# Two blocks in float32 by split operands: where the low part of the down projections' weights is made

## Chip, cores and metric

One core of one Trainium2 chip. The metric is the device time of one execution in microseconds, from the hardware profiler; two executions of the kernel before gave 1640.35 and 1642.58 us, their median is 1641.46 us.

## What is computed

256 tokens of 1024 channels go through two blocks. The first has a gated feed-forward layer, a hybrid mixer (attention in a window and pooled means), a second feed-forward layer and a gated embedding, each with an RMS norm ahead and behind. The second has two rounds of feed-forward, mixer (gated linear attention in the first round, retention in the second) and feed-forward, each followed by a layer norm. Six of these layers are the same feed-forward, with a hidden width of 2816:

```python
def swiglu(x, w_gate, w_up, w_down):
    return (jax.nn.silu(x @ w_gate) * (x @ w_up)) @ w_down

for i in range(DEPTH_2):
    h = layer_norm(DN_ALPHA * h + 0.5 * swiglu_2(h, ffn_w_in[i, 0], ffn_w_out[i, 0]), ln_g[i, 0], ln_b[i, 0])
    ...
    h = layer_norm(DN_ALPHA * h + 0.5 * swiglu_2(h, ffn_w_in[i, 1], ffn_w_out[i, 1]), ln_g[i, 2], ln_b[i, 2])
```

The loop is the second block's, whose `swiglu_2` is the same with gate and up in one matrix. All data is float32, and so is the result.

## The kernel before

**Split operands.** The matmuls take float32r operands, to which a copy rounds. Each float32 operand is therefore two tiles: a high part, the operand rounded to float32r, and a low part, the operand minus its high part. A product is three matmuls into the same PSUM tile: high by high, high of the tokens by low of the weight, low of the tokens by high of the weight (`mm3`, lines 173 to 177). Each has 128 rows, 128 columns of tokens and 512 columns of weight.

**Weights.** They come from HBM in 275 units of 128 x 2048 float32 (1 MB), in the order of `all_units`. `fetch` (line 143) makes one unit ready: SP starts the load into a `raw` tile (L154), ScalarE writes the rounded copy to `whi` (L155), VectorE writes `raw - whi` to `wlo` (L156). There are 4 `raw` tiles and 5 each of `whi` and `wlo` (`BUFS`, line 94); a tile is written again once the last reader of its former content is done. A feed-forward layer has 12 units of gate, 10 of up and 11 of down, which stand one behind another in the plan; the six layers' down units (`f1d`, `f2d`, `s0d` to `s3d`) are 66 of the 275. They are called d0 to d10 here.

**Down projection** (`lagged`, line 296). The tokens are two blocks of 128, t = 0 and t = 1. Unit i of down is used for t = 0 in step i and for t = 1 three units later (`LAG = 3`): step i does 12 matmuls of t = 0 on unit i, then 12 of t = 1 on unit i-3. So four units are held at any time and the fifth tile is the only one that can be filled ahead. The last two units' work for t = 1 comes at the very end. `after(0)`, the norm of the first block of tokens and the transposes for the next layer, follows t = 0's last step and lies beside the rest of t = 1's products; then comes `after(1)`.

**Order of work.** The source calls `fetch` for unit i+1 when unit i is taken up (`unit`, line 159). The tile framework takes the source's order as priority only: when the program is built it goes through it with durations of its own and writes down for each engine, TensorE too, what can start next by these. So an engine's queue is not always in the source's order; on the chip the queues are fixed, and each engine takes its own strictly in order. Waits are put in by the framework where one engine needs what another wrote, or overwrites what another reads.

**GpSimd** has only small work: parts of the norms (L204, L205, L219, L281) and some element-wise products of the mixers. It starts no DMA in this kernel. The framework keeps a scratch for DMA descriptors of GpSimd's, which is set to 1024 bytes per partition (`dynamic_dma_scratch_size`, line 1011).

Of the kernel before, what the change touches and what calls it, by code (L numbers as in the profile page):

```python
# [11 lines left out]
F32 = mybir.dt.float32  # L12
# [3 lines left out]
ALU = mybir.AluOpType  # L16
# [18 lines left out]
AHEAD = 2  # L35
TURN = (5, 7)


class Split:
    """A float32 operand as two float32r tiles that add up to it exactly."""  # L40

# [7 lines left out]
def ffn_units(g, u, d):  # L49
    """Five chunks of 512 columns of gate and up; their last 256 columns share gate's last two units."""  # L50
    out = []
    for c in range(5):
        out += [(g, 2 * c), (g, 2 * c + 1), (u, 2 * c), (u, 2 * c + 1)]
    return out + [(g, 10), (g, 11)] + [(d, i) for i in range(11)]
# [11 lines left out]
def all_units():  # L66
    """Every weight unit in the order of its use."""
    p = ffn_units("f1g", "f1u", "f1d")
    p += chunk_units("bin", MIX_ORDER) + [("bpl", 0), ("bat", 0), ("bpl", 1), ("bat", 1)] + [("bout", i) for i in range(4)]
    p += ffn_units("f2g", "f2u", "f2d")  # L70
    p += [("pgate", i) for i in range(4)] + [("pproj", 0)]
    p += ffn_units("s0g", "s0u", "s0d")
    p += chunk_units("gin", GLA_ORDER) + [("gout", i) for i in range(4)]
    p += ffn_units("s1g", "s1u", "s1d") + ffn_units("s2g", "s2u", "s2d")
    p += chunk_units("rin", RET_ORDER) + [("rout", i) for i in range(8)]
    return p + ffn_units("s3g", "s3u", "s3d")


class Build:
# [4 lines left out]

# [1 line left out]
    def open(self, ctx):  # L86
# [31 lines left out]
    def const(self, name, i, n=CW, dt=F32):  # L118
        """Piece i of a constant, [128, n]."""
        c = self.T("ld", [P, CW], dt, name=name)  # L120
        self.nc.sync.dma_start(out=c[:, :n], in_=self.ins[name][i])
        return c[:, :n]

# [1 line left out]
    def tick(self):  # L125
        """Six products of 512 columns have gone out: what waited for them follows."""
        self.clock += 1
        while self.later and self.later[0][0] <= self.clock:
            self.later.pop(0)[2]()

    def defer(self, n, fn):
        """Issue fn after n more ticks."""
        self.seq += 1
        self.later.append((self.clock + n, self.seq, fn))
        self.later.sort(key=lambda e: e[:2])

    def settle(self, done):
        """Issue what waits until done()."""
        while not done():
            self.later.pop(0)[2]()  # L140

# [1 line left out]
    def fetch(self, fine=False):  # L143
        """The plan's next unit, on its way to be split."""
        nc = self.nc
        name, i = self.plan[len(self.ready)]
        raw = self.T("raw", [P, UNIT], F32)
        hi = self.T("whi", [P, UNIT], F32R)
        lo = self.T("wlo", [P, UNIT], F32R)
        parts = 4 if fine else 1  # L150
        n = UNIT // parts
        for j in range(parts):
            s = slice(j * n, (j + 1) * n)
            nc.sync.dma_start(out=raw[:, s], in_=self.ins[name][i][:, s])  # L154
            nc.scalar.copy(hi[:, s], raw[:, s])  # L155
            nc.vector.tensor_tensor(out=lo[:, s], in0=raw[:, s], in1=hi[:, s].bitcast(F32), op=ALU.subtract)  # L156
        self.ready.append(Split(hi, lo))

    def unit(self, name, i, kb, ahead=1):
        """Unit i of a weight, on chip and split, as kb rows of blocks."""  # L160
        assert self.plan[self.taken] == (name, i), (name, i, self.plan[self.taken])
        self.taken += 1
        self.ahead(ahead)
        w = self.ready[self.taken - 1]
        self.ready[self.taken - 1] = None
        v = lambda x: x.rearrange("p (k n) -> p k n", k=kb)
        return Split(v(w.hi), v(w.lo))
# [10 lines left out]

# [1 line left out]
    def transpose4(self, src, n=4, name="tp"):  # L180
        """src: [128, n*128] in SBUF -> PSUM [128, n*128], each block transposed."""
        ps = self.TP(name)
# [4 lines left out]
    def split(self, src, n=4, name="xT"):  # L187
        """[128, n*128] -> Split of [128, n, 128]."""
        hi = self.S([P, n, P], F32R, name + "h")
# [8 lines left out]

# [1 line left out]
    def rpow(self, v, eps, n=1, name="r"):  # L200
        """(v + eps) ** -0.5"""
        e = self.small(n, "e" + name)
# [5 lines left out]
    def sumsq(self, srcs, scale):  # L208
        """Sum over the row of (scale * src) ** 2, each source on its own."""
        st = self.small(len(srcs), "ss")  # L210
# [15 lines left out]

# [1 line left out]
    def row_rstd(self, t):  # L228
# [3 lines left out]
    def rms_in(self, t, gpre):  # L232
        """The next layer's operand from h[t]: h * g, transposed and split, and its rstd."""
        nc, h = self.nc, self.h[t]
# [8 lines left out]
    def turn_in(self, xT, t, n, u):  # L243
        """xT[n] becomes u's transpose, once u is about to be there."""
        self.defer(TURN[t] + n, lambda: xT.__setitem__(n, self.splitT(u)))

    def rms_post(self, t, acc, gpost, half):
        """h[t] += (0.5 if half else 1) * rms_norm(acc) * g"""
        nc, h = self.nc, self.h[t]
# [8 lines left out]
    def ln_post(self, t, acc, g, b, half, last=False):  # L258
        """h[t] = layer_norm(ALPHA * h + (0.5 if half else 1) * acc) * g + b; its transpose, split."""
        nc, h = self.nc, self.h[t]  # L260
# [22 lines left out]

# [1 line left out]
    def proj(self, ps, x, w, n=CW, kb=4, k0=0, nk=None):  # L285
        """ps[128, n] += x @ w for one block of tokens; x: list of Split [128, 4, 128], w: list of units
        from row of blocks k0 on, of nk in all."""
        nk = nk or kb * len(w)
# [7 lines left out]
    def lagged(self, x, name, n_units, after, lag=LAG, have=None, extra=None):  # L296
        """[256, K] @ [K, 1024], the first block of tokens ahead of the second by `lag` units of two rows
        of blocks. after(t, acc) follows each block's end; extra: what else follows a step."""
        lag = min(lag, n_units)
# [84 lines left out]
    class Chunks:  # L384
        """x @ w in chunks of 512 columns, issued in pieces of half a unit: a chunk's end calls done(c, t, ps).
        The first two chunks go block of tokens by block of tokens, the others unit by unit."""

# [33 lines left out]

# [1 line left out]
    def mixer(self, xT, r, after):  # L423
# [134 lines left out]

# [1 line left out]
    def ple(self, xT, r, gpost, after):  # L560
# [27 lines left out]

# [1 line left out]
    def gla(self, xT, after):  # L590
# [90 lines left out]
        def inner(t):  # L681
            """The weights of a block of tokens on itself: within each chunk, and of its second chunk on its first."""
            ps, over = self.M("sT"), self.TP("sTo")
# [12 lines left out]
        def far():  # L696
            """The first block's keys decayed to its end, and the second block's queries from its start."""
            e = v3(E1[0])[:, :, P - 1:].to_broadcast([P, H, C])
# [7 lines left out]
        def carry(hp):  # L706
            """What the first block of tokens leaves to the second, for a pair of heads."""
            ps = self.M("kv")
# [36 lines left out]

# [1 line left out]
    def ret(self, xT, after):  # L747
# [76 lines left out]

# [1 line left out]
    def run(self, ctx):  # L826
# [7 lines left out]

        # the first operand comes transposed; its gain is a scalar of each row
        g0 = self.T("g0", [P, KD])
# [28 lines left out]
        def rms_layer(body, post, half, pre):  # L865
            """One residual layer of block 1; the next one's operands."""
            g = {}
# [45 lines left out]
def units(w, kb, n):  # L913
    """[K, N] -> [units, 128, kb * n]: columns outer, rows inner."""
    k, nn = w.shape
# [4 lines left out]
def units_ff(g, u):  # L920
    """Units of gate and of up; the last 256 columns of both make the last two of gate's."""
    last = np.concatenate([g[:, 2560:], u[:, 2560:]], 1)
# [3 lines left out]
def constants():  # L926
    """What depends on shapes alone."""
    out = {"ident": np.eye(P, dtype=np.float32)}
# [25 lines left out]
def bias_windows(rpb):  # L954
    """[8, 15, 31] -> [(t, pair, a), 128 queries, (j, 256 keys)], NEG outside of the window."""
    cols = np.arange(64)
# [65 lines left out]
```

## Time and profile before

| | us |
|---|---|
| two executions, and their median | 1642.58, 1640.35; 1641.46 |
| span of the profiled execution, first to last instruction | 1639.3 |
| TensorE busy with matmuls | 1622.8 |
| VectorE busy | 935.0, of it 632.4 in L156 |
| ScalarE busy | 723.9, of it 526.9 in L155 |
| GpSimd busy | 131.1 |

The median lies 2.2 us above the profiled span. A duration in the rows is from the instruction's start to its end; a matmul's row is longer than the distance to the next one, as they overlap. "Idle before" is the time that the engine had nothing under way, with what ended it.

### The profile page before, as it was taken

The page shows a single profiled execution, that of the slowest core. Times are in us where ns is not written, and L with a number is a line of the kernel's source. Part 1 is how long each engine was busy: PE and PEld are TensorE (multiplying, and loading weights), DVE is VectorE, ACT ScalarE, POOL GpSimd, SP SyncE. Part 2 cuts the span into 40 slices and gives each one's busy share as a digit, 9 for nine tenths or more (in the row PEclk, how much of TensorE's full clock was granted, in tenths as well). Part 3 has the DMA queues.
Part 4 walks back from the last instruction along what each step waited for, and adds up shares of the span by engine and source line. Part 5 has one row for each costly group of instructions (what it writes and reads, how often), then busy time and mean ns, then how long its engine had stood idle before and what let it go on. Part 6 is the DMA issues. An engine that isn't in the chain of part 4 may idle for free.

```text
span 1639.3 us, 18199 instructions
## 1 busy us (share of the span) xinstructions
PE 1622.8 (99%) x7512; PEld 1339.8 (82%) x7512; DVE 935.0 (57%) x809; ACT 723.9 (44%) x712; POOL 131.1 (8%) x149
## 2 busy tenths in 40 slices
PE   8999999999999999999999999999999999999997
PEld 6888878888888888888888888888887888888886
DVE  6644665565453864537747544654538666485444
ACT  6443554454443754333644433443424444344331
POOL 0000200020000300003011000100003300010000
PEclk9999999999999999999999999999999999999999
DMA  9754654545454564546535454555445544364540
GB/s 356 266 184 154 227 210 143 180 176 210 178 193 158 210 229 177 205 146 214 190 138 213 175 203 149 192 223 206 165 169 206 215 154 166 142 240 172 204 150 30
DMA packets 49650, 308.09 MB, mean 188 GB/s; under 512 B 6032, under 2 KB 7056, under 8 KB 14880
## 3 DMA queue, kind: packets, MB, share of 16 engines
q1 hardware_dynamic: 49568, 306.94, 51.6%
q8 instruction: 59, 0.97, 0.2%
q14 instruction: 23, 0.19, 0.0%
HBM read 305.86 MB, written 1.05 MB: 187 GB/s over the span
## 4 chain that ended last, share of the span: by engine, by line
PE 96%; DVE 2%; issue 1%; ACT 0%; DMA 0%; POOL 0%; DVEq 0%; POOLq 0%; SPq 0%
PE mm L175 21%; PE mm L177 21%; PE mm L176 20%; PE acc L177 9%; PE acc L175 9%; PE acc L176 9%; PE hT L184 2%; DVE wlo L156 1%; PE xT L184 1%; PE tp L184 1%; PE sc L464 1%; PE o L487 0%; DVE bn L265 0%; DVE h L264 0%; PE sT L795 0%
## 5 line engine op out<-in xcount | busy, mean ns | idle before, releaser
L156 DVE TENSOR_TENSOR wlo<-raw,whi 128x2048 fp32r<-128x2048 f32 (+1 forms) x287 | 632.4, 2209 | 481.4 <-ACT whi L155 481.3
L155 ACT CAST whi<-raw 128x2048 fp32r<-128x2048 f32 (+1 forms) x287 | 526.9, 1841 | 558.6 <-PE mm L177 283.3
L175 PE MATMUL mm<-whi,xTh 128*128 128x512 f32 x1296 | 516.4, 398 | 0.0
L177 PE MATMUL mm<-whi,xTl 128*128 128x512 f32 x1296 | 506.0, 391 | 0.5 <-DVE xTl L193 0.5
L176 PE MATMUL mm<-wlo,xTh 128*128 128x512 f32 x1296 | 505.0, 390 | 0.0
L177 PEld LDWEIGHTS mm<-whi,xTl 128*128 128x128 f32 x1296 | 243.2, 188 | 53.3 <-DVE xTl L193 1.3
L175 PEld LDWEIGHTS mm<-whi,xTh 128*128 128x128 f32 x1296 | 243.4, 188 | 50.5 <-issue 2.7
L176 PEld LDWEIGHTS mm<-wlo,xTh 128*128 128x128 f32 x1296 | 243.8, 188 | 47.6
L175 PE MATMUL acc<-whi,hTh 128*128 128x512 f32 x528 | 207.4, 393 | 0.0
L177 PE MATMUL acc<-whi,hTl 128*128 128x512 f32 x528 | 205.7, 390 | 0.0
L176 PE MATMUL acc<-wlo,hTh 128*128 128x512 f32 x528 | 205.6, 389 | 0.0
L177 PEld LDWEIGHTS acc<-whi,hTl 128*128 128x128 f32 x528 | 99.1, 188 | 20.7
L176 PEld LDWEIGHTS acc<-wlo,hTh 128*128 128x128 f32 x528 | 99.2, 188 | 20.1
L175 PEld LDWEIGHTS acc<-whi,hTh 128*128 128x128 f32 x528 | 99.1, 188 | 19.8
L193 DVE TENSOR_TENSOR hTl<-hT,hTh 128x512 fp32r<-128x512 f32 (+1 forms) x72 | 46.3, 643 | 58.8 <-ACT hTh L192 58.8
L175 PE MATMUL mm<-whi,xh 128*128 128x512 f32 x176 | 70.5, 401 | 6.6 <-ACT whi L155 6.6
L176 PE MATMUL mm<-wlo,xh 128*128 128x512 f32 x176 | 69.6, 395 | 0.0
L177 PE MATMUL mm<-whi,xl 128*128 128x512 f32 x176 | 69.4, 394 | 0.0
L204 POOL TENSOR_SCALAR erl<-mv 128x1 f32<-128x1 f32 x12 | 5.1, 423 | 771.5 <-DVE mv L267 771.5
L344 ACT ACTIVATE sg<-mm 128x512 f32<-128x512 f32 (+1 forms) x48 | 26.9, 560 | 86.9 <-issue 56.6
L219 POOL TENSOR_TENSOR v<-ss 128x1 f32<-128x1 f32 x16 | 16.2, 1016 | 529.3 <-ACT jk L213 529.3
L192 ACT CAST hTh<-hT 128x512 fp32r<-128x512 f32 (+1 forms) x72 | 39.3, 546 | 26.0 <-PE hT L184 26.0
(216 smaller groups left out, 1267.4 us busy)
## 6 DMA issues: line engine op xcount, KB each, us to landing
raw<-in_rin SPq DMA_DIRECT2D x24, 1024.0 KB, 4.8
raw<-in_bin SPq DMA_DIRECT2D x16, 1024.0 KB, 4.8
raw<-in_f2g SPq DMA_DIRECT2D x12, 1024.0 KB, 4.8
raw<-in_s0g SPq DMA_DIRECT2D x12, 1024.0 KB, 4.9
raw<-in_gin SPq DMA_DIRECT2D x12, 1024.0 KB, 4.8
raw<-in_s1g SPq DMA_DIRECT2D x12, 1024.0 KB, 4.8
raw<-in_s2g SPq DMA_DIRECT2D x12, 1024.0 KB, 4.8
raw<-in_s3g SPq DMA_DIRECT2D x12, 1024.0 KB, 4.8
```

The lines of the kernel that those rows point to most:

```text
L155: nc.scalar.copy(hi[:, s], raw[:, s])
L156: nc.vector.tensor_tensor(out=lo[:, s], in0=raw[:, s], in1=hi[:, s].bitcast(F32), op=ALU.subtract)
L175: mm(ps, x.hi, w.hi, start=start, stop=False)
L176: mm(ps, x.hi, w.lo, start=False, stop=False)
L177: mm(ps, x.lo, w.hi, start=False, stop=stop)
L184: self.nc.tensor.transpose(ps[:, i * P:(i + 1) * P], src[:, i * P:(i + 1) * P], self.ident)
L192: self.nc.scalar.copy(hi, v)
L193: self.nc.vector.tensor_tensor(out=lo, in0=v, in1=hi.bitcast(F32), op=ALU.subtract)
L204: self.nc.gpsimd.tensor_scalar(out=e, in0=v, scalar1=1.0, scalar2=eps, op0=ALU.mult, op1=ALU.add)
L219: self.nc.gpsimd.tensor_tensor(out=v, in0=st[:, 0:1], in1=st[:, 1:2], op=ALU.add)
L344: nc.scalar.activation(sg[:, :n], ps_g[:, :n], AF.Silu)
L464: nc.tensor.matmul(ps[:, j * SEQ:(j + 1) * SEQ], qT[t][64 * a:64 * a + 64, 2 * b + j, :], kT[b][64 * a:64 * a + 64, j, :], start=True, sto ...
```

## The change

Down units no longer take VectorE's subtraction. SP loads `raw` and ScalarE writes `whi` as before. Then a second ScalarE pass writes minus `whi` to `wlo`, and GpSimd starts a DMA from `raw` to `wlo` (both on chip, 1 MB) that adds what it reads to what lies there. All other units are made as before. Removed comments and docstrings change nothing; lines behind the edit move by up to 8.

```diff
 TURN = (5, 7)
+DOWN = ("f1d", "f2d", "s0d", "s1d", "s2d", "s3d")
...
     def fetch(self, fine=False):
...
         raw = self.T("raw", [P, UNIT], F32)
         hi = self.T("whi", [P, UNIT], F32R)
         lo = self.T("wlo", [P, UNIT], F32R)
+        if name in DOWN:
+            nc.sync.dma_start(out=raw, in_=self.ins[name][i])
+            nc.scalar.copy(hi, raw)
+            nc.scalar.activation(lo, hi.bitcast(F32), AF.Copy, scale=-1.0)
+            nc.gpsimd.dma_start(out=lo.bitcast(F32), in_=raw, accum_op=ALU.add)
+            self.ready.append(Split(hi, lo))
+            return
         parts = 4 if fine else 1
```

## Rows read from the trace of the kernel before

**Rows 1.** The profile's page: span, and engines' busy time, share, instructions.

```profile
span 1639.3 us, 18199 instructions
...
PE 1622.8 (99%) x7512; PEld 1339.8 (82%) x7512; DVE 935.0 (57%) x809; ACT 723.9 (44%) x712; POOL 131.1 (8%) x149
```

**Rows 2.** Waits of TensorE: who for whom, us in total, times, longest.

```profile
PE mm L175 <- ACT whi L155: 6.6, 1, 6.6
PE xT L184 <- DVE y L276: 1.1, 3, 0.4
PE mm L177 <- DVE xTl L193: 0.5, 1, 0.5
```

**Rows 3.** Groups by shape: the split of whole units; busy us, mean ns.

```profile
L156 DVE TENSOR_TENSOR wlo<-raw,whi 128x2048 fp32r<-128x2048 f32 x271 | 622.2, 2299 | 479.9 <-ACT whi L155 479.8
L155 ACT CAST whi<-raw 128x2048 fp32r<-128x2048 f32 x271 | 517.7, 1913 | 554.3 <-PE mm L177 283.3 <-PE acc L177 212.6 <-issue 42.1
```

**Rows 4.** Timeline of ScalarE around the first down projection: start, us, instruction.

```profile
119.28 1.91 ACT L155 CAST whi<-raw 128x2048 fp32r<-128x2048 f32 x1 [5.62 <-PE mm L177]
122.04 1.91 ACT L155 CAST whi<-raw 128x2048 fp32r<-128x2048 f32 x1 [0.86 <-PE mm L177]
...
127.98 0.47 ACT L347 ACTIVATE sg<-mm,rs 128x256 f32<-128x256 f32 x1 [3.54 <-issue]
...
131.12 1.91 ACT L155 CAST whi<-raw 128x2048 fp32r<-128x2048 f32 x1 [2.17 <-PE mm L177]
...
147.95 1.91 ACT L155 CAST whi<-raw 128x2048 fp32r<-128x2048 f32 x1 [7.82 <-PE acc L177]
153.43 1.91 ACT L155 CAST whi<-raw 128x2048 fp32r<-128x2048 f32 x1 [3.57 <-PE acc L177]
...
175.15 1.91 ACT L155 CAST whi<-raw 128x2048 fp32r<-128x2048 f32 x1 [3.53 <-PE acc L177]
...
182.63 0.60 ACT L213 ACTIVATE jk<-acc 128x512 f32<-128x512 f32 x1
```

**Rows 5.** Timeline of VectorE: the subtraction of the unit copied at 153.43.

```profile
155.38 2.29 DVE L156 TENSOR_TENSOR wlo<-raw,whi 128x2048 fp32r<-128x2048 f32 x1 [3.19 <-ACT whi L155]
```

**Rows 6.** Timeline of TensorE: kernel's start, down's first matmul, next layer's.

```profile
6.58 0.80 PE L175 MATMUL mm<-whi,xh 128*128 128x512 f32 x1 [6.58 <-ACT whi L155]
...
10.88 0.63 PE L175 MATMUL mm<-whi,xh 128*128 128x512 f32 x1
11.31 0.43 PE L176 MATMUL mm<-wlo,xh 128*128 128x512 f32 x1
...
133.78 0.48 PE L175 MATMUL acc<-whi,hTh 128*128 128x512 f32 x1
...
194.93 0.39 PE L175 MATMUL mm<-whi,xTh 128*128 128x512 f32 x1
```

**Rows 7.** Stretches: us, busy time (and instructions) by engine, clock, DMA share, GB/s.

```profile
20.00:24.00 4.00, 4.00 (x19) 3.33 (x18) 0.32 (x1) 3.47 (x10) 0.97 (x4) 1.00 1.04 422
133.80:199.00 65.20, 65.20 (x295) 53.96 (x293) 32.76 (x23) 28.78 (x29) 8.74 (x9) 1.00 0.49 178
```

**Rows 8.** DMA queue: packets, MB, share; a down unit's load: count, KB, landing us.

```profile
q1 hardware_dynamic: 49568, 306.94, 51.6%
...
raw<-in_f1d SPq DMA_DIRECT2D x11, 1024.0 KB, 4.8
```

**Rows 9.** Waits of SP's queue for `raw` tiles: us in total, times, longest.

```profile
SPq L154 <- DVE wlo L156: 1270.3, 252, 15.2
```

**Rows 10.** Groups by shape: a small GpSimd instruction of the norms.

```profile
L219 POOL TENSOR_TENSOR v<-ss 128x1 f32<-128x1 f32 x16 | 16.2, 1016 | 529.3 <-ACT jk L213 529.3
```

## Prediction

> **What bounds the kernel now.** I began with the page [rows 1]: TensorE is busy 1622.8 us of 1639.3, VectorE 57% and ScalarE 44%. Then TensorE's waits [rows 2]: 6.6 us before its first matmul and 1.6 us in all the rest. So the matmuls' sequence is the bound; what the change takes off VectorE can give back those 1.6 us and no more, while whatever makes TensorE wait is added in full. 2% of the median is 33 us, about what a measurement of this kernel can tell from no change, so a gain of that size is excluded by these rows.
>
> The next question is how much room a down unit has between the release of its tiles and its use. ScalarE's timeline shows it [rows 4]: from 147.95 on the copies of d5 to d10 each wait for `PE acc`, the last reader of the tile that they overwrite. From 153.43 to 175.15 are four units, so one step of TensorE (24 matmuls) takes 5.43 us; 5.44 is used below. Unit i+5's tile is released at the end of step i+3, step i+4 runs, and step i+5 needs the high part at once and the low part one matmul (0.23 us) later. The room is 5.44 + 0.23 = 5.67 us. Before, the copy takes 1.91 and the subtraction begins 1.95 us behind the copy's start and lasts 2.29 [rows 4, 5]: 4.24 us, and 1.4 to spare. That is why VectorE's work costs nothing now.
>
> **The change part by part.**
>
> *Removed:* 66 subtractions of 2.30 us [rows 3], 152 us of VectorE. They were covered by the matmuls: worth 0 to 1.6 us; I take 0.
>
> *Added on ScalarE:* 66 passes over 128 x 2048, from SBUF to SBUF as the copy, so by its row 1.91 us each [rows 3], 126 us in all, which takes ScalarE from 44 to 52%. Behind it in the queue stand the next layer's and the last chunk's small passes; ScalarE idles 3.5 us and more before each copy of the down stage [rows 4], which hides them; with no such cover the 126 us would be paid. In the chain of a unit, the pass with its step from one to the next is 1.95 us.
>
> *Added on GpSimd:* 66 DMA issues. No row shows one; the nearest is a small instruction of the norms, 1.0 us [rows 10]. A DMA issue on SP's side is no nearer kind of work, so 0.2 to 3 us; I take 1.0, and each us of it moves the sum by 3 x 6 = 18. Each issue waits for ScalarE's pass, and what is queued behind it on GpSimd is the norm's small work, which comes a unit or more later: nothing, or 1 us for a layer if it came at once.
>
> *Added on the DMA engines:* 66 accumulating transfers of 1 MB. None is in the trace of before, so it is bounded by loads. Loads that fill the engines move 422 GB/s [rows 7], 2.5 us for 1.05 MB; in the down stage the share is 0.49 of 5.44 us, 2.7 us for one load [rows 7]; over the kernel 51.6% of the span for 306.94 MB is 2.9 [rows 8]. I use 2.6 us of all 16 engines for one pass. A load lands 4.8 us after its issue [rows 8], so 1.9 us to 2.3 are latency; I use 1.9. An accumulating transfer reads `raw`, reads `wlo` and writes `wlo`, where a load reads once and writes once. Lower end: one pass, 2.6. Upper end: three passes, 7.8, if nothing overlaps. I take two reads for one, 5.2, which lies between and is twice the nearest row.
>
> *The wait that this makes.* From the release to the low part: 1.95 (copy) + 1.95 (second pass) + 1.0 (issue) + 5.2 + 1.9 = 12.0 us. The engines are not free meanwhile: each accumulate that ends frees a `raw` tile, SP waits for exactly that now (1270 us, on the subtraction [rows 9]) and starts the next load, so about one load, 2.6 us, lies beside each accumulate: 14.6 us. Against a room of 5.67 TensorE is 8.9 us late at d5. d6's tile was released a step before, at the same distance, so with 8.9 more of room it comes about in time; d7's tile is released only at the end of d5's step, and is 8.9 late again; so is d9. That is 3 x 8.9 = 26.8 us for a down stage. The earlier units: copies of d1 and d2 start at 119.28 and 122.04, 17 us before their use, and are covered. d3's copy starts at 131.12 [rows 4] and its step at 133.78 [rows 6] + 3 x 2.72 (three half steps) + 0.44 of transposes, 142.4, with the 0.23 a room of 11.5, so 3.1 us late; d4's has room through that. So 29.9 us for each of the first five feed-forward layers. In the last there is no next layer to load for: 3 x (12.0 - 5.67) + 0.5 = 19.5. Sum: 5 x 29.9 + 19.5 = 169 us.
>
> A second way to the same term is a budget of the DMA engines. d1's accumulate can't start before 119.28 + 3.9 + 1.0 = 124.2. Up to d10 are ten accumulates (52 us) and some nine loads (23 us), then 1.9 of latency: 201 against d10's turn at 180.5 (142.4 + 7 x 5.44), 21 us late whatever the order of the matmuls. 6 x 21 = 126: the forecast's own floor.
>
> *Weighing a rule.* In the rows all data goes by one queue [rows 8], and loads behind one another fill the engines (share 1.04 [rows 7]); no row shows two queues at once. By the Trainium skill, DMA: Bandwidth & Descriptors, section Issuing engines are not separate DMA queues, transfers issued by GpSimd run on the same 16 engines as SP's and interleave with them. By it the sum is the 169 as it stands. Were GpSimd's transfers to run beside SP's without taking from them, each late unit would be late by 6.3, and the sum 6 x 19.5 = 117 us. No run here shows which yet.
>
> The sum: the profiled 1639.3 + 169 + the 2.2 by which the median lies above that span = **1810 us**.
>
> **Rivals.**
>
> *A, the latency goes under (not slower).* The queues are ordered at the build by what the framework takes to be ready. The rows show that it leaves the source's order: d1's and d2's copies stand ahead of the activation of chunk 5 at 127.98 [rows 4], though the source fetches d1 behind it. If it knows that the low part comes late, it can put work of t = 1 ahead of t = 0's next unit. Five tiles turn over in 5 x 5.44 = 27.2 us, and a chain of 9.4 (one pass) plus 5.44 fits into that, so TensorE need not wait. The lag then shrinks from three units to about two, and the cover of the norm behind t = 0 with it: from ScalarE's first pass of the norm at 182.63 [rows 4] to the next layer's first matmul at 194.93 [rows 6] TensorE had just enough of t = 1 to do. A loss of 2 us for a layer: 1641.5 + 12 = 1653. It decides from the engines' budget: 124.2 + 23 + 1.9 + 10 accumulates must be under 180.5, so an accumulate may cost 3.1 us of the engines, near the lower end. Against it: twice as much is read as by a load.
>
> *B, the accumulate costs three passes or more.* By the same budget 124.2 + 78 + 23 + 1.9 = 227, 47 us late; 6 x 47 = 282: 1923. For it: nothing in the trace shows such a transfer overlapping its two sides.
>
> *C, TensorE's clock falls in the new gaps.* At the start TensorE has been idle for 6.58 us, and its first ten matmuls, from 6.58 to 11.31 [rows 6], take 4.7 us; the tenth is 0.43 us ahead of the next, which is 512 columns at 1.2 GHz. Ten take 2.3 us (10 x 5.43 / 24) in the down stage, where the granted clock reads 1.00 [rows 7], the level of 2.4 GHz. So a restart costs 2.4 us. With four gaps of 3 to 9 us in each of six stages that is 24 x 2.4 = 58 us more: 1868. Against it: part of that hides behind the next wait for DMA. The Trainium skill, TensorE: Matmul & The Clock Gate, Part 1, says that the clock falls after idleness and comes back with activity; the trace agrees at the start, and no run here shows gaps of this length later on.
>
> *D, a cheaper mix:* order partly turned, accumulate of 3 to 4 us: 5 to 15 us a layer, 1672 to 1730.
>
> **How the numbers follow.** Forecast (two passes; from the floor of 126 to some 60 above the sum where the gaps of the first four units add up, so 1765 to 1870): 0.50. A (within 2%): 0.13. B (over 1900): 0.18. C on top of the forecast, around 1868 and more: 0.09. D: 0.08, which is slower by over 2% but for its lowest end. Faster by over 2%: 0.02, for what no row shows. The range reaches from A's 1655 to beyond B, 1950. Slower by over 2%: 0.50 + 0.18 + 0.09 + 0.08 = 0.85; within 2%: 0.13.
>
> **What would show it.** Right: TensorE's waits name the accumulating DMA or `wlo` before L176's weight loads, some four a feed-forward layer of 3 to 9 us; the window of a down stage has a DMA share near 1 where it was 0.49; GpSimd's issues land 8 us and more later; SP waits for the accumulate instead of L156. L155 and gate and up stay as they are. A would show TensorE busy 97% or more with wider spacing between t = 0's units, B a landing of over 10 us with the engines full, C matmuls 0.43 us apart behind gaps. The forecast is wrong if TensorE's waits in the down stages sum to under 33 us, or if they stand at other places: on ScalarE's second pass, or at the norms.

## The result, and the profile after

The changed kernel takes 1802.23 and 1802.59 us in two executions, median 1802.41, against 1641.46 before: 1.097 times the time, interval 1.095 to 1.100. It is slower, by 161 us. The profiled execution has a span of 1800.1 us, 160.8 more than before.

The page, the lines that answer to [rows 1] and [rows 8] (engines; DMA queues with packets, MB, share of the 16 engines):

```profile
span 1800.1 us, 18394 instructions
...
PE 1673.5 (93%) x7512; PEld 1363.6 (76%) x7512; DVE 785.7 (44%) x743; ACT 847.9 (47%) x778; POOL 185.7 (10%) x215
...
q1 hardware_dynamic: 49568, 306.94, 46.2%
q0 software_dynamic: 9504, 69.21, 19.4%
```

VectorE lost 149 us and ScalarE gained 124, as meant, and the time follows neither. TensorE's matmuls are the same 7512, yet their busy time rose by 50.7 us (1673.5 - 1622.8), and its idle time rose by the rest. The queue q0 is new: 66 accumulating transfers, 19.4% of the span, 5.3 us of all 16 engines each (0.194 x 1800.1 / 66).

Waits of TensorE, which answer to [rows 2], then SP's, which answer to [rows 9] (us in total, times, longest):

```profile
PE acc L184 <- DMA wlo<-raw: 103.6, 35, 6.6
...
PE mm L183 <- ACT whi L163: 6.9, 1, 6.9
...
PE xT L192 <- DVE y L284: 4.2, 5, 1.0
```

```profile
SPq L162 <- DVE wlo L164: 853.9, 175, 15.2
SPq L152 <- DMA wlo<-raw: 360.8, 42, 12.7
```

The first line of the first is the result: TensorE waits 35 times, 103.6 us in all, and always for the accumulating DMA, ahead of a matmul with the low part of a down unit (`acc`, L184, which was L176). ScalarE's passes and VectorE's split of the other units stand in no such line but the kernel's start. SP now waits for the accumulate before it loads the next unit: this answers to the subtraction of [rows 9].

The groups, as in [rows 3] (busy us, mean ns, then idle before), and DMA issues (count, KB, median us to landing):

```profile
L184 PE MATMUL mm<-wlo,xTh 128*128 128x512 f32 x1296 | 505.0, 390 | 0.0
...
L184 PE MATMUL acc<-wlo,hTh 128*128 128x512 f32 x528 | 225.6, 428 | 103.6 <-DMA wlo<-raw 103.6
L185 PE MATMUL acc<-whi,hTl 128*128 128x512 f32 x528 | 220.5, 420 | 0.0
...
L154 ACT ACTIVATE wlo<-whi 128x2048 fp32r<-128x2048 f32 x66 | 126.5, 1916 | 2.1
```

```profile
wlo<-raw POOLq DMA_DIRECT2D x66, 1024.0 KB, 10.0
...
raw<-in_f1d SPq DMA_DIRECT2D x11, 1024.0 KB, 6.2
```

ScalarE's second pass costs what the copy costs (1916 ns for 1913 in [rows 3]). These matmuls of the down stage take 428 and 420 ns where those of gate and up (`mm`) still take 390: something slows them in these stages. At the median an accumulate lands 10.0 us after its issue; a load of the first down stage landed after 4.8 us before [rows 8] and lands after 6.2 now.

GpSimd's timeline of the first down stage, then TensorE's at four of the five waits (start, us, instruction, idle before and its releaser):

```profile
136.16 0.89 POOL L155 DMA_DIRECT2D wlo<-raw  x1 [6.81 <-ACT hTh L200]
140.54 0.88 POOL L155 DMA_DIRECT2D wlo<-raw  x1 [3.49 <-PE hT L192]
160.76 0.86 POOL L155 DMA_DIRECT2D wlo<-raw  x1 [19.35 <-ACT wlo L154]
...
170.15 0.89 POOL L155 DMA_DIRECT2D wlo<-raw  x1 [2.93 <-ACT wlo L154]
```

```profile
149.51 0.79 PE L184 MATMUL acc<-wlo,hTh 128*128 128x512 f32 x1 [6.00 <-DMA wlo<-raw]
...
167.74 0.50 PE L184 MATMUL acc<-wlo,hTh 128*128 128x512 f32 x1 [2.02 <-DMA wlo<-raw]
...
185.00 0.80 PE L184 MATMUL acc<-wlo,hTh 128*128 128x512 f32 x1 [3.79 <-DMA wlo<-raw]
...
202.45 0.50 PE L184 MATMUL acc<-wlo,hTh 128*128 128x512 f32 x1 [2.26 <-DMA wlo<-raw]
```

d3's accumulate, issued at 136.16, ends TensorE's wait at 149.51, 13.3 us later; d4's was issued 4.4 us behind it and ran beside it, d2's was under way until 140.0, and two loads, issued at 134.51 and 140.09, took 10.5 and 12.3 us to land. d5's, issued at 160.76 with no other accumulate beside it until 166.35, ends a wait 7.0 us later. d7's, issued at 170.15 with d6's, d8's and two loads beside it, ends one after 14.8 us. Over the six stages the waits for d3 and d7 make 62.7 of the 103.6 us; these accumulates took 13.0 to 15.5 us, and the DMA engines' share was 0.99 to 1.03 meanwhile.

Stretches around the first wait and the whole first stage (us, busy time and instructions by engine, granted clock, DMA share, GB/s), which answer to [rows 7]:

```profile
140.00:145.00 5.00, 3.52 (x17) 2.54 (x15) 0.42 (x1) 0.55 (x2) 0.88 (x1) 1.00 0.99 226
145.00:150.00 5.00, 0.49 (x1) 0.49 (x2) 0.00 (x0) 0.00 (x0) 0.00 (x0) 0.59 1.02 288
150.00:155.00 5.00, 5.00 (x18) 3.89 (x18) 0.00 (x0) 0.00 (x0) 0.00 (x0) 0.73 1.03 288
...
133.00:215.00 82.00, 65.95 (x256) 51.74 (x255) 6.21 (x6) 35.88 (x26) 8.39 (x11) 0.88 0.94 253
```

In the 5 us behind the gap TensorE does 18 matmuls where full pace is 22 (24 in 5.44 us), at a granted clock of 0.73, and the DMA engines are full. Over the whole stage their share is 0.94. The chain of waits shows the matmuls one by one (start, us):

```profile
136.16 13.31 DMA wlo<-raw
149.51 0.79 PE acc L184
150.31 0.43 PE acc L185
...
152.44 0.40 PE acc L184
152.84 0.24 PE acc L185
153.09 0.23 PE acc L183
```

0.43 us is the pace at 1.2 GHz that the kernel's start showed [rows 6]; from 152.84 on it is 0.23. So the 160.8 us of the span are 103.6 of waits for accumulates, 50.7 of slower matmuls, and 6.5 left over, part of it at the norms' `xT` waits.

### The profile page after: what moved, and what is told of

Read it like the earlier page. It is cut to its first block, busy times and chain, and to the rows that moved or that the text cites. A ratio compares the mean times of both kernels' runs of the same rounds, so it can differ in the third digit from the quotient of the medians.

```text
span 1800.1 us, 18394 instructions
## 1 busy us (share of the span) xinstructions
PE 1673.5 (93%) x7512; PEld 1363.6 (76%) x7512; DVE 785.7 (44%) x743; ACT 847.9 (47%) x778; POOL 185.7 (10%) x215
## 3 DMA queue, kind: packets, MB, share of 16 engines
q0 software_dynamic: 9504, 69.21, 19.4%
## 4 chain that ended last, share of the span: by engine, by line
PE 77%; DMA 13%; issue 6%; DVE 2%; ACT 1%; POOL 1%; POOLq 0%; DVEq 0%; SPq 0%; ACTq 0%
PE mm L183 19%; PE mm L184 19%; PE mm L185 18%; DMA wlo<-raw 13%; PE acc L184 5%; PE acc L185 5%; PE acc L183 4%; PE hT L192 1%; DVE wlo L164 1%; PE xT L192 1%; ACT whi L163 1%; PE tp L192 1%; PE sc L472 0%; PE o L495 0%; DVE h L272 0%
## 5 line engine op out<-in xcount | busy, mean ns | idle before, releaser
L164 DVE TENSOR_TENSOR wlo<-raw,whi 128x2048 fp32r<-128x2048 f32 (+1 forms) x221 | 481.4, 2184 | 606.6 <-ACT whi L163 545.3
L163 ACT CAST whi<-raw 128x2048 fp32r<-128x2048 f32 (+1 forms) x221 | 400.5, 1817 | 366.1 <-PE mm L185 227.1
L185 PE MATMUL mm<-whi,xTl 128*128 128x512 f32 x1296 | 505.5, 391 | 0.0
L184 PE MATMUL mm<-wlo,xTh 128*128 128x512 f32 x1296 | 505.0, 390 | 0.0
L184 PE MATMUL acc<-wlo,hTh 128*128 128x512 f32 x528 | 225.6, 428 | 103.6 <-DMA wlo<-raw 103.6
L185 PEld LDWEIGHTS mm<-whi,xTl 128*128 128x128 f32 x1296 | 243.2, 188 | 53.1 <-DVE xTl L201 1.0
L184 PEld LDWEIGHTS mm<-wlo,xTh 128*128 128x128 f32 x1296 | 243.8, 188 | 47.5
L153 ACT CAST whi<-raw 128x2048 fp32r<-128x2048 f32 x66 | 126.0, 1909 | 260.9 <-PE acc L185 220.3
L185 PE MATMUL acc<-whi,hTl 128*128 128x512 f32 x528 | 220.5, 420 | 0.0
L184 PEld LDWEIGHTS acc<-wlo,hTh 128*128 128x128 f32 x528 | 108.1, 205 | 142.2 <-DMA wlo<-raw 119.7
L155 POOL DMA_DIRECT2D wlo<-raw x66 | 57.7, 874 | 1026.2 <-ACT wlo L154 978.6
L154 ACT ACTIVATE wlo<-whi 128x2048 fp32r<-128x2048 f32 x66 | 126.5, 1916 | 2.1
L185 PEld LDWEIGHTS acc<-whi,hTl 128*128 128x128 f32 x528 | 108.9, 206 | 22.8
L183 PEld LDWEIGHTS acc<-whi,hTh 128*128 128x128 f32 x528 | 107.6, 204 | 24.2
L184 PE MATMUL mm<-wlo,xh 128*128 128x512 f32 x176 | 69.7, 396 | 0.0
L185 PE MATMUL mm<-whi,xl 128*128 128x512 f32 x176 | 69.6, 396 | 0.0
```

Source lines behind the costliest of these rows:

```text
L153: nc.scalar.copy(hi, raw)
L154: nc.scalar.activation(lo, hi.bitcast(F32), AF.Copy, scale=-1.0)
L155: nc.gpsimd.dma_start(out=lo.bitcast(F32), in_=raw, accum_op=ALU.add)
L183: mm(ps, x.hi, w.hi, start=start, stop=False)
L184: mm(ps, x.hi, w.lo, start=False, stop=False)
L185: mm(ps, x.lo, w.hi, start=False, stop=stop)
```

## The experiments

Each run is set against the kernel before on the same chip. A diff is against the changed kernel unless it says otherwise. Two theories stood at the start: that a unit's **chain** (copy, pass, issue, transfer) is longer than the room that the tiles leave, and that the **budget** of the DMA engines is overdrawn. A third question was what the falling clock adds. The expectations call the chain T2 and the budget T1.

**Is it the passes and the queue, or the transfer?** ScalarE's second pass stays, VectorE's subtraction overwrites what it wrote:

```diff
-            nc.gpsimd.dma_start(out=lo.bitcast(F32), in_=raw, accum_op=ALU.add)
+            nc.vector.tensor_tensor(out=lo, in0=raw, in1=hi.bitcast(F32), op=ALU.subtract)
```

> ScalarE's second pass is kept, but VectorE's subtraction writes the low part after it, and there is no accumulate: what the added 126 us of ScalarE cost by themselves. Main theory (they lie in ScalarE's idle time; the chain is 1.95 + 1.95 + 2.29 = 6.2 us against a room of 5.67, which the turned order of the matmuls takes up): 1640 to 1650 us. Rival (ScalarE's queue delays the activations and the norms): 10 us and more in a layer, over 1700 us.

Measured: 1646.17 us, ratio 1.0025 (1.0015 to 1.0036). 66 more passes of ScalarE, with VectorE behind them, cost 5 us: TensorE's weight loads now wait 20 times for VectorE's subtraction of a down unit, at most 0.4 us each and 6.5 us in all. And only units d0 to d2 by accumulate, whose tiles are free long before their use:

```diff
-        if name in DOWN:
+        if name in DOWN and i < 3:
```

> Only d0, d1 and d2 of each stage go by the accumulate (their tiles are released 17 us before their use), the other eight by VectorE. Both theories: the accumulates end in time and load the engines in a stretch that is half empty: 1640 to 1648 us. Were the mere presence of accumulating transfers or of GpSimd's issues harmful, 18 of 66 would cost 18/66 of 161 us, 44 us: 1685 us.

Measured: 1644.79 us, 1.0019 (1.0009 to 1.0028). TensorE's waits for an accumulate, and the landing:

```profile
PE acc L184 <- DMA wlo<-raw: 0.8, 1, 0.8
```

```profile
wlo<-raw POOLq DMA_DIRECT2D x18, 1024.0 KB, 9.7
```

At the median they land hardly sooner than in the changed kernel, and yet they cost 0.8 us of waits and 3.6 us of the time. So neither the transfer's presence nor GpSimd's issue is the price; the units whose tiles are released late pay it.

**How much the addition costs.** The same transfer without the addition, so that the low part is the raw unit:

```diff
-            nc.gpsimd.dma_start(out=lo.bitcast(F32), in_=raw, accum_op=ALU.add)
+            nc.gpsimd.dma_start(out=lo.bitcast(F32), in_=raw)
```

> Left out: the addition (the DMA overwrites the low part with the raw unit); all queues stand in the same order as in the changed kernel. Theory T1 (the 16 DMA engines are full, because the accumulate reads twice, 5.3 us of them for a unit): one read instead of two brings a unit to about 2.6 us of the engines, the budget up to d10 fits again (124 + 26 + 23 + 2 = 175 against 180), the landing falls from 10 us to 5 to 6, and the time to 1645 to 1675 us. Rival T2 (the length of the chain from GpSimd's issue, not the engines' load): the landing stays over 8 us and the time over 1720 us. T3 (the clock): wherever TensorE's waits go, the matmuls at 0.43 us go too.

Measured: 1725.95 us, 1.0522 (1.0494 to 1.0549). Queue and landing:

```profile
q0 software_dynamic: 9504, 69.21, 10.1%
...
wlo<-raw POOLq DMA_DIRECT2D x66, 1024.0 KB, 6.8
```

0.101 x 1732.5 / 66 = 2.65 us of the engines, half of the accumulate's 5.3: the size of two passes in the prediction was right. But the time didn't fall to the 1645 to 1675 of the budget. With half the transfer TensorE still waits 51.1 us for it: 3.9 us of passes and 6.8 to land, or the 4.8 of the one issued at 151.96 with nothing beside it, are over the room of 5.67. This speaks for the chain, though the landing that the chain's expectation named, over 8 us, didn't come.

**Extra load on the engines.** Half a MB more per down unit, into a tile that nobody reads:

```diff
             nc.sync.dma_start(out=raw, in_=self.ins[name][i])
+            aux = self.T("aux", [P, 1024], F32)
+            nc.sync.dma_start(out=aux, in_=self.ins[name][i][:, :1024])
```

> The changed kernel with 0.5 MB more loaded for each down unit into a tile that nobody reads (1.3 us of the engines); matmuls in the same order. T1 (budget of the engines): all of it is added from d1 on, 10 to 11 x 1.3 us in each of six stages, 78 to 86 us more: 1880 to 1890 us. T2 (chain): only the late units d5, d7 and d9 get longer, 3 x 1.3 x 6 = 23 us: about 1825 us.

Measured: 1821.67 us, 1.1092 (1.1076 to 1.1109), 19 us over the changed kernel, landing 10.3 us for 10.0. Were the engines' budget the bound, 66 halves of 2.6 us would have been paid in full, 86 us. They are not; the chain's 1825 is met within 4 us.

**One pass less in the chain.** The low part begins from `raw`, ahead of the copy, so that the accumulate needn't wait for the copy:

```diff
-            nc.scalar.copy(hi, raw)
-            nc.scalar.activation(lo, hi.bitcast(F32), AF.Copy, scale=-1.0)
+            nc.scalar.activation(lo, raw, AF.Copy, scale=-1.0)
             nc.gpsimd.dma_start(out=lo.bitcast(F32), in_=raw, accum_op=ALU.add)
+            nc.scalar.copy(hi, raw)
```

> The negative high part is rounded straight from the raw unit, ahead of the copy: the accumulate can start 1.95 us sooner, the engines' work stays. T1 (budget): only the start of the row of accumulates moves, 2 us for a stage, 12 us: 1785 to 1795 us. T2 (chain): 3 x 1.95 us for a stage, 35 us: 1760 to 1770 us.

Measured: 1784.43 us, 1.0859 (1.0832 to 1.0885): 18 us less, between the 12 and the 35 of the expectation, and so it doesn't tell them apart. TensorE's waits for accumulates fell from 103.6 to 89.6 us, still 35 times.

**Half the columns.** Columns 1024 to 2047 by accumulate, the others by VectorE:

```diff
-            nc.scalar.activation(lo, hi.bitcast(F32), AF.Copy, scale=-1.0)
-            nc.gpsimd.dma_start(out=lo.bitcast(F32), in_=raw, accum_op=ALU.add)
+            a, b = slice(0, UNIT // 2), slice(UNIT // 2, UNIT)
+            nc.vector.tensor_tensor(out=lo[:, a], in0=raw[:, a], in1=hi[:, a].bitcast(F32), op=ALU.subtract)
+            nc.scalar.activation(lo[:, b], hi[:, b].bitcast(F32), AF.Copy, scale=-1.0)
+            nc.gpsimd.dma_start(out=lo[:, b].bitcast(F32), in_=raw[:, b], accum_op=ALU.add)
```

> Only columns 1024 to 2047 of a down unit are made by the accumulate, the others by VectorE's subtraction: half the engines' work (2.6 us), a chain of 1.95 + 1.0 + 0.9 + 2.6 + 1.9 = 8.4 us and more with a load beside it; matmuls in the source's order. T1 alone (budget): 124 + 26 + 23 + 2 = 175 against 180, no loss, 1642 to 1655 us. T2 (chain against a room of 5.67 us): 2.7 to 5.3 us late at three units of a stage, 48 to 95 us more: 1690 to 1737 us.

Measured: 1719.7 us, 1.0467 (1.0431 to 1.0503), and TensorE's waits:

```profile
PE acc L186 <- DMA wlo<-raw: 51.7, 27, 3.4
```

The chain's forecast was at least 3 waits of 2.7 us in 6 stages, 49; the sum came, but in 27 waits of 1.9 us. The engines had room here (2.9 us an accumulate, a share of 0.74 from 133 to 200), so by the budget alone nothing would be lost: waits come without an overdrawn budget.

**Room enough.** With a lag of one unit in place of three, two units are held and three tiles fill ahead. The same edit on the kernel before is the control, since a smaller lag also takes cover from the norms:

```diff
-        self.lagged(lambda t, k: hT[t, k // 4][:, k % 4, :], wd, 11, after, have=lambda t, k: (t, k // 4) in hT)
+        self.lagged(lambda t, k: hT[t, k // 4][:, k % 4, :], wd, 11, after, lag=1, have=lambda t, k: (t, k // 4) in hT)
```

> The changed kernel with t = 1 one unit behind t = 0 in the down stage instead of three, so that two more tiles are free for units ahead: room 16 us. T2 (chain): the waits for the low part go, and the time is that of the kernel before with the same lag, give or take 10 us. T1 (budget of the engines): the row of accumulates is as long as ever; d10 comes at 201 against a turn of about 186, 15 us late in a stage: some 90 us above the kernel before with the same lag.

> Control: the kernel before with a lag of one unit in the down stage. The norm behind t = 0 then has 5.4 us of products beside it where it had 10.9, so up to 5.4 us for a layer are lost: 1641 + 6 x 2 to 6 x 5.4 = 1653 to 1674 us.

Measured: 1754.77 us, 1.0689 (1.0673 to 1.0704); the control 1661.08, 1.0119 (1.0103 to 1.0136). A stretch of the first down stage, and the accumulates' landing, of the run with accumulates:

```profile
133.00:200.00 67.00, 57.29 (x238) 44.52 (x236) 4.53 (x5) 33.69 (x21) 6.99 (x8) 0.97 1.02 278
```

```profile
wlo<-raw POOLq DMA_DIRECT2D x66, 1024.0 KB, 13.2
```

The DMA engines are full for the whole stage (1.02), an accumulate lands after 13.2 us, and TensorE waits 42 times, at most 3.2 us, 63.4 in all. This is the budget as the bound, once the chain isn't: 94 us above the control, about the 90 expected. So the budget would be left if the chain fitted. In the changed kernel the two overlap: its waits for d3 and d7 stand behind transfers that full engines stretched to twice the 6.9 us of one by itself. How much of the 103.6 us would go if nothing lay beside these was not measured.

**Does the built order matter?** In the changed kernel TensorE's queue isn't in the source's order: work of t = 1 stands ahead of parts of t = 0's next unit. Here the down stage's matmuls are held to the source's order:

```diff
         mm = self.nc.tensor.matmul
+        if self.pin:
+            mm = lambda *a, **kw: self.tc.keep_in_program_order(self.nc.tensor.matmul(*a, **kw))
...
+        self.pin = True
         self.lagged(lambda t, k: hT[t, k // 4][:, k % 4, :], wd, 11, after, have=lambda t, k: (t, k // 4) in hT)
+        self.pin = False
```

> The changed kernel with the down stages' matmuls pinned to the source's order (all of t = 0's unit i, then all of t = 1's unit i-3). If the chain against the tile's release sets the loss, as the forecast's sum has it: 3 x (14.3 - 5.7) us at d5, d7 and d9 and some 7 us at d3, about 33 us for a stage, 198 us of waits, and up to 50 us by the clock: 1840 to 1890 us, so the turned order saved 40 to 90 us. If the engines' budget alone sets it, the order doesn't matter: 1795 to 1810 us.

Measured: 1844.5 us, 1.1243 (1.1225 to 1.1262). The turned order was worth 42 us, at the lower end of the 40 to 90 expected; of the two parts expected, 198 us of waits and up to 50 by the clock, 137.0 and 62.5 came. This kernel is the clean case of the prediction's working. TensorE's waits, its timeline at the four of the first stage, the chain at the second, and SP's loads before and behind it:

```profile
PE acc L185 <- DMA wlo<-raw: 137.0, 32, 6.3
```

```profile
146.66 0.79 PE L185 MATMUL acc<-wlo,hTh 128*128 128x512 f32 x1 [5.45 <-DMA wlo<-raw]
...
166.15 0.79 PE L185 MATMUL acc<-wlo,hTh 128*128 128x512 f32 x1 [5.57 <-DMA wlo<-raw]
...
184.59 0.80 PE L185 MATMUL acc<-wlo,hTh 128*128 128x512 f32 x1 [5.52 <-DMA wlo<-raw]
...
203.95 0.80 PE L185 MATMUL acc<-wlo,hTh 128*128 128x512 f32 x1 [5.67 <-DMA wlo<-raw]
```

```profile
154.95 1.91 ACT L154 CAST whi<-raw 128x2048 fp32r<-128x2048 f32 x1 [16.31 <-PE acc L185]
156.89 1.92 ACT L155 ACTIVATE wlo<-whi 128x2048 fp32r<-128x2048 f32 x1
```

```profile
159.17 6.94 DMA wlo<-raw
```

```profile
153.76 0.33 SPq L153 DMA_DIRECT2D raw<-in_f1d  x1
...
166.16 0.33 SPq L153 DMA_DIRECT2D raw<-in_f1d  x1
```

Four waits in the stage, at every second unit, as worked out: d3, d5, d7, d9. From the copy's start to the landing, d5 takes 166.11 - 154.95 = 11.2 us; less the room of 5.67 that is 5.5, and 5.57 is measured. No load lies beside this transfer: the one of 153.76 landed 4.7 us later, and the next starts when TensorE's wait is over. The same four units wait in every stage, 24 waits of 4.4 to 6.3 us that make 132.4 of the 137.0; the other eight are under 1.2 us each. (The held matmuls all have the line of the edit, L185.)

**Does the falling clock cost what it seems to?** The last kernel with 12 matmuls ahead of the low part's first matmul at d3, and 24 at d5, d7 and d9, into a PSUM tile that nobody reads:

```diff
         mm(ps, x.hi, w.hi, start=start, stop=False)
+        if self.fill:
+            spare = self.TP("fill")
+            for _ in range(self.fill):
+                mm(spare, x.hi, w.hi, start=True, stop=True)
+            self.fill = 0
...
+            if self.pin and (t, n, k) == (0, 0, 2 * u):
+                self.fill = {3: 12, 5: 24, 7: 24, 9: 24}.get(u, 0)
```

> The same pinned order, with products of high parts into a PSUM tile that nobody reads put where the gaps are: 12 matmuls (2.7 us) ahead of d3's first use of its low part, 24 each (5.4 us) ahead of d5's, d7's and d9's. They fit into gaps of 7 to 9 us. If the clock's fall behind a gap adds to the time, TensorE's pace stays at 0.23 us and the time falls by up to 18 to 24 x 2.4 = 43 to 58 us below the pinned order without them. If slower matmuls behind a gap hide in the next wait for the DMA, the time stays within 10 us. If the fillers cost by themselves, it grows by up to 6 x 19 = 114 us.

Measured: 1859.28 us, 1.1323 (1.1303 to 1.1344), 15 us more than without them. The fall of 43 to 58 didn't come, nor did the time stay within 10. TensorE's timeline of the first stage, at two of the fillings (24 matmuls in a row) and the waits behind them:

```profile
161.20 5.60 PE L185 MATMUL fill<-whi,hTh 128*128 128x512 f32 x24
...
174.20 0.50 PE L185 MATMUL acc<-wlo,hTh 128*128 128x512 f32 x1 [1.60 <-DMA wlo<-raw]
...
179.79 5.60 PE L185 MATMUL fill<-whi,hTh 128*128 128x512 f32 x24
...
193.40 0.69 PE L185 MATMUL acc<-wlo,hTh 128*128 128x512 f32 x1 [2.56 <-DMA wlo<-raw]
```

No wait stands at d5 and d7 any more. But now one stands a unit later, at d6 (174.20), d8 (193.40) and d10, 1.6 to 3.1 us. In the run before, TensorE took 7.2 us from d5's low part to d6's, the first matmuls of it at half pace, and that gave d6's accumulate, which took 8.7 us from its issue, the time to land. In the filled run the same accumulate takes 8.8 us, and TensorE is at d6's low part 5.7 us behind d5's, too early. So this run shows that slower matmuls and waits partly stand in for one another. How much the kernel would gain at a clock that never falls it doesn't settle: the fillings also take their own time where a gap is shorter than they are.

Where each run's span went, against the 1639.3 us, 1622.8 of matmuls and no wait for accumulates of the kernel before (us; "matmuls" is TensorE's busy time; the last column is what the two ahead of it leave; the spans are of the profiled executions, that of the plain copy 8.7 us slower than its median):

| run | span | waits for accumulates | matmuls | rest |
|---|---|---|---|---|
| changed kernel | +160.8 | 103.6 | +50.7 | 6.5 |
| second pass only | +5.2 | 0 | +5.4 | -0.2 |
| d0 to d2 only | +4.2 | 0.8 | +1.6 | 1.8 |
| plain copy | +93.2 | 51.1 | +36.4 | 5.7 |
| half the columns | +77.5 | 51.7 | +26.0 | -0.2 |
| minus `raw` first | +142.2 | 89.6 | +51.5 | 1.1 |
| extra load | +180.0 | 118.0 | +54.4 | 7.6 |
| lag 1 | +112.3 | 63.4 | +30.8 | 18.1 |
| kernel before, lag 1 | +19.5 | 0 | +7.8 | 11.7 |
| source's order | +200.0 | 137.0 | +62.5 | 0.5 |
| source's order, filled | +213.2 | 58.7 | +153.1 | 1.4 |

In the last row some 114 us of the matmuls are the 504 fillings (5.44 / 24 us each). Not all of the matmuls' column is the clock: short waits of the weight loads stand in it too, as the second row suggests, where the clock read 0.999 as before. None of the runs beats the kernel before. TensorE waited 1.6 us in it behind its start, so the low part's maker had nothing to give, and no faster version was tried.

## Why the prediction was right, and where its steps were not

**The bound** held. 149 us off VectorE gave nothing back, and what makes TensorE wait is paid in full.

**The mechanism** held: a chain longer than the room of 5.67 us makes TensorE wait in all six down stages, with GpSimd's issue and ScalarE's pass at no place of their own in TensorE's waits. Its pattern, every second unit from d3 on, is that of the source's order; in the changed kernel's own order the first stage waits at d3, d5, d6, d7 and d9. The parts were: pass 1.92 us (1.95 with its step), from the pass's end to the issue's row 0.37 and 0.87 for the issue itself (1.0 had been taken), engines 5.3 (5.2 taken), issue to landing 6.94 where nothing lies beside (1.0 + 5.2 + 1.9 = 8.1 taken with the issue in it), which leaves some 0.8 of latency for the 1.9 taken.

**The predicted 1810 met 1802 by two sizes that were off in opposite directions.** The sum had 169 us of waits and none for the clock; measured were 103.6 and 50.7. That the two come within 8 us of the forecast is luck.

*The waits, 169 for 103.6.* First, the step "about one load, 2.6 us, lies beside each accumulate: 14.6 us" failed for d5, d7 and d9 in the source's order. A load can start only when an accumulate has ended, for it needs that `raw` tile. So there it doesn't lie beside the late unit's accumulate, which lands in 6.9 to 7.4 us, but beside the next one, which has time to spare. This makes 11.2 - 5.67 = 5.5 us a wait where 8.9 had been worked out. Second, d3 is no lighter than the others: 5.45 us against the 3.1, as d2's and d4's accumulates and two loads run beside d3's, which takes 12.5 to 13.6 us in the six stages. 24 waits of 5.5 are 132, and the source's order has 137. Third, TensorE's queue isn't in the source's order. The turning brought 33 us of that back (137.0 to 103.6), though it puts two accumulates and two loads beside d7's, which takes 14.1 to 15.5 us there for 7.0 in the source's order. This is what rival A put as its mechanism; the prediction let it decide only below 3.1 us an accumulate, and it gave a part at 5.3.

*The clock, none for 50.7.* Rival C priced a restart at 2.4 us from the kernel's start and had 58 us for 24 gaps. In the source's order, where there are 24 gaps of some 5.5 us and eight short ones, the matmuls take 62.5 us longer, 2.6 for each of the 24; in the changed kernel with its shorter gaps 50.7. The term belonged into the forecast, not beside it. Its 1868 wasn't reached because it was put on top of the 169. The Trainium skill, TensorE: Matmul & The Clock Gate, section HAM oscillation, describes matmuls in short bursts between waits for DMA that begin at the low clock each time; the stretch behind the first wait agrees, with a granted clock of 0.73 and 18 matmuls where 22 fit. The objection in the prediction, that part of the loss hides behind the next wait, is what the filled run shows.

*The budget's floor, 126*, was too high: 94 us with lag 1 against its control, 16 a stage where 21 had been worked out. The engines' price of an accumulate in it was right; what it had too much of stays open.

*The rule weighed* (one set of engines for both queues) holds: with both queues at work the share stands at 0.99 to 1.03 around the first wait, no higher than with loads alone (1.04 [rows 7]), and each queue slows the other: the two loads beside d3's accumulate land after 10.5 and 12.3 us where it was 4.8, and d3's accumulate, beside these and two others, after 13.3 where one alone takes 6.9. That the 117 worked out for queues that don't disturb each other lies near the measured 103.6 is a chance: it stood for the source's order, and that has 137.

**Rivals.** A (1653) fell: an accumulate takes 5.3 us of the engines where A wanted 3.1. B (three passes) fell by the same number. D had a partly turned order, as it came, but with a transfer of 3 to 4 us, and fell by that. C's mechanism was there, as told.

**What would show it**: TensorE's waits name the accumulate, five in the first stage and 35 in all six; the DMA share of the stage rose from 0.49 to 0.94; landing is over 8 us at the median; SP waits for the accumulate. All were seen, but for the sizes: some four waits of 3 to 9 us a stage had been named, and 11 of the 35 are over 3 us. The sign named for C, matmuls 0.43 us apart behind the gaps, was seen as well, so the signs didn't part the forecast from C.

## What to carry to other kernels

Before an on-chip transfer takes the place of an engine's pass, set its whole way, from the release of its tile to its landing, against the time in which the ring of tiles comes round; an engine with time to spare is no reason by itself. Ask of each load where it lies: a load that needs what a transfer frees can't lie beside that transfer, but it can lie beside the next. And where TensorE will get gaps of several us, add the restart of its clock to the sum from a row that shows one, but look whether the next wait swallows a part.

## What the runs showed of the hardware that was not expected

- An accumulating transfer between two SBUF tiles takes twice the DMA engines' time of the plain copy, 5.3 against 2.65 us for 1 MB. The Trainium skill, Collectives: The Full Stack, section The bandwidth ceiling, tells of a reduction that it needs two source reads where a copy needs one, and so runs at half the rate; these two runs agree with the half, 5.3 / 2.65, on a transfer within one core; that the second read is the reason they don't show. Half a unit takes 2.9 us of the engines, a little over half.
- Alone an accumulate lands after 6.9 us and the plain copy after 4.8, though the copy takes half as much of the engines. With two other accumulates and two loads beside it, one accumulate took 13.3.
- 24 gaps of some 5.5 us cost 2.6 us each of slower matmuls behind them, as the 6.58 us at the kernel's start cost 2.4. Short gaps aren't always free of it: behind the 2.3 us gap that ends at 202.45 in the changed kernel, TensorE goes on at full pace for some matmuls and then falls to the low one (granted clock 0.77 from 205 to 210), as the chain shows. Behind the 2.0 us gap that ends at 167.74 it doesn't fall (1.00 from 165 to 175).

```profile
202.45 0.50 PE acc L184
202.95 0.24 PE acc L185
...
203.66 0.23 PE acc L183
203.89 0.31 PE acc L184
204.21 0.43 PE acc L185
```
